# Three edits in the attention stage of a two-layer hybrid backbone: when bias tables are loaded, how a scan operand is laid out, and how many modulation products share an accumulator

## The chip, the cores and the metric

The kernel runs on one core of a Trainium2 chip. The time is device microseconds (us) of one execution; the number for the kernel before is the median of three runs. Rows of a trace come from one further execution, taken by the hardware profiler.

## The reference, cut to what matters

A backbone of two layers works on 1024 latent tokens and 256 context tokens of width 1024. Each layer computes six modulation vectors from two conditioning vectors, normalises the tokens, projects them into four head groups of width 256, mixes each group in its own way, and adds the projected result back; then a gated MLP follows. The three things that the change touches are these:

```
mod = split(silu(c) @ ada_w[l] + ada_b[l], 6)                    # 1024 x 6144 product, two rows
s_lat = q_r @ k_r.T * scale + bias ; s_lat = where(mask, s_lat, NEG_INF)   # neighbourhood heads
S = S*w_t + (S @ a_t) outer b_t + v_t outer k_t ; y_t = S @ r_t  # the scan, both directions
```

All results are float32, and one output of 1024 x 1024 is written.

## The kernel before, in words

**How the order is made.** The program is written as Python generators that are pulled in turns. A planner (the context is opened with `schedule_with_timeline_sim=True`) then fixes, at build time, the order of the instructions on each engine and on SP's queue, which issues all DMAs: of the instructions that its own model holds for ready, it takes the one that the program emitted first. An instruction that waits for nothing, as a load into a free buffer, can so come long before its place in the program. On the chip each engine works through its list in the planned order.

**The stage around the change.** `mix` first runs the dense projections and the preparation of the scan. Then it opens the attention units (`attn_open`, `units`, `unit_events`): per layer 8 units of the differential group, 20 or 16 of the latent group, and last 20 or 16 of the neighbourhood group (`na_unit`). A unit is 128 queries of a head pair: scores on PE (`sl`), row maxima on DVE (`rl`), exponentials on ACT (`ex`), transposes on PE (`tr`, into one of two `psT` buffers), products with V (`pv`), and an output DMA to `ymix` (L1068). While they run, `tick` pulls three side jobs at fixed rates: `scan` (`rw_step_gen`, rate 0.8), `ada` (`ada_gen`, rate 0.2, so one pull in five ticks) and, once `ada` has ended, `rwo` (`rw_out_gen`, rate 0.5, it ends with the stores at L784). Another job, `lanes_gen`, still does small DVE products (L547, L548) when the stage begins. The stage ends in the output projection, which reads `ymix` back.

**Bias.** In `na_unit`, `load()` brings Q (L865; three Q buffers, so a Q load waits until an earlier unit has let go) and calls `bias()` when the unit has another bias type than the one before. `bias()` loads a mask `msk` (L847, one buffer) and two bias tables `nb` (L850, two buffers) and adds the mask on POOL (L852, two additions). DVE uses them in the row maximum (L957). Each layer loads ten biases.

**Scan.** `rw_step_gen` does 20 steps per layer in sequence. A step multiplies on PE (L664, eight products, 128-row operands), copies the result to `Dt` on ACT (L667, 128 partitions), multiplies again (L676, eight products, each with operands of 64 rows, one half of the partitions for each head e of a pair), copies that result into the zero-padded `V1` in two halves, ACT for partitions 0 to 63 (L678) and DVE for 64 to 127 (L679), multiplies (L688), and updates the state on DVE (L696). POOL prepares `V1` and `stmp` (L660, L670) for it. The operands of a segment come by DMA (VS L629, SG L630, XB L631).

**Modulation.** `ada_gen` loads weights of 512 KB (L1535, three buffers), multiplies each (L1556, four column groups) and adds the 128x256 result to a row: ACT copies the first of eight (L1561), DVE adds the others (L1563). `adg` says how many of the eight accumulate in PSUM before the row is touched: here 1. The accumulator comes from `psT`. 48 weights are used in the first layer's stage, 32 in the second's; a load for weight j+3 is emitted right after the product of weight j.

Of the kernel before, what the change touches and what calls it, by code (L numbers as in the profile page):

```python
# [9 lines left out]
F32 = mybir.dt.float32  # L10
F32R = mybir.dt.float32r
AF = mybir.ActivationFunctionType
# [5 lines left out]
P = 128  # L18
# [22 lines left out]
class K:  # L41
# [561 lines left out]
    def rw_step_gen(self, l, pool, sgp, yp, psp, ptag, need_ctx, F):  # L603
        nc = self.nc
        TT, ACT, MM = nc.vector.tensor_tensor, nc.scalar.activation, nc.tensor.matmul
        segs = ([8, 9] + list(range(8)), [9, 8] + list(range(8))[::-1])
        sg = {}

        def need(i):
            return max(self.SLOT.index(segs[d][i]) for d in range(2))  # L610

        def step_y(i):
            return i >= 2 or need_ctx

        SZ = pool.tile([P, 2, 2, 2, 64], F32, name="SZ", bufs=1)
        for e in range(2):
            nc.gpsimd.memset(SZ[64 - 64 * e:128 - 64 * e, e], 0.0)

        def seg(i):
            SG = sgp.tile([P, 2, 1792], F32, tag="SG", name="SG", bufs=2)  # L620
            XB = pool.tile([P, 2, 4, 64], F32, tag="XB", name="XB", bufs=2)
            VS = pool.tile([P, 2, 2, 2, 2, 64], F32, tag="VS", name="VS", bufs=2)
            W = pool.tile([P, 2, 2, 2], F32, tag="W", name="W", bufs=2)
            for d in range(2):
                sl = self.SLOT.index(segs[d][i])
                vt = self.rvt[sl, d].rearrange("(c s) e p i -> e s c (p i)", c=2)
                for e in range(2):
                    q = slice(64 - 64 * e, 128 - 64 * e)
                    nc.sync.dma_start(VS[q, :, e, d].rearrange("s c p i -> s c (p i)"), vt[e])  # L629
                nc.sync.dma_start(SG[:, d], self.rsg[sl, d])  # L630
                nc.sync.dma_start(XB[:, d].rearrange("p u t -> p (u t)"), self.rxf[sl, d].rearrange("p u c t -> p (u c t)"))  # L631
                nc.gpsimd.tensor_copy(W[:, :, d], self.Wc[:, sl, d].rearrange("p (a c) -> p c a", a=2))
            if i == 0:
                for e in range(2):
                    nc.gpsimd.memset(VS[64 * e:64 * e + 64, 0, e], 0.0)
            BT = SG[:, :, 0:512].rearrange("p d (e u t) -> p d e u t", e=2, u=4)
            RB = SG[:, :, 512:768].rearrange("p d (u t) -> p d u t", u=4)
            ARM = SG[:, :, 768:1792].rearrange("p d (e u t) -> p d e u t", e=2, u=4)
            sg[i] = (XB, RB, BT, ARM, W, VS)

        while F["lanes"] <= need(0):
            yield
        seg(0)
        for _ in range(3):
            yield
        for step in range(20):
            i, c = step // 2, step % 2
            if c == 1 and i + 1 < 10:
                while F["lanes"] <= need(i + 1):
                    yield  # L650
            if c == 0 and i + 1 < 10 and F["lanes"] > need(i + 1):
                seg(i + 1)
            XB, RB, BT, ARM, W, VS = sg[i]
            V1 = pool.tile([P, 2, 2, 2, 64], F32, tag="V1", name="V1", bufs=2)
            pall = psp.tile([P, 2, 2, 2, 64], F32, tag=ptag, name="pall")
            pd, psa = pall[:, 0], pall[:, 1]
            tmp = pool.tile([P, 2, 2, 64], F32, tag="stmp", name="stmp", bufs=1)
            for e in range(2):
                q = slice(64 - 64 * e, 128 - 64 * e)
                nc.gpsimd.tensor_copy(V1[q, e], VS[q, c, e])  # L660
            for d in range(2):
                for p in range(2):
                    for e in range(2):
                        MM(pd[64 * e:64 * e + 64, d, p], ARM[:, d, e, 2 * p + c, 0:64], VS[:, c, e, d, p], start=True, stop=True)  # L664
            yield
            Dt = pool.tile([P, 2, 2, 64], F32, tag="Dt", name="Dt", bufs=2)
            ACT(Dt, pd, AF.Copy)  # L667
            for e in range(2):
                r = slice(64 * e, 64 * e + 64)
                nc.gpsimd.tensor_tensor(out=tmp[r], in0=VS[r, c, e], in1=W[r, c, :, :, None].to_broadcast([64, 2, 2, 64]), op=ALU.mult)  # L670
            yield
            for d in range(2):
                for p in range(2):
                    for e in range(2):
                        r = slice(64 * e, 64 * e + 64)
                        MM(psa[r, d, p], XB[r, d, 2 * p + c], Dt[r, d, p], start=True, stop=True)  # L676
            yield
            ACT(V1[0:64, 0], psa[0:64], AF.Copy)  # L678
            nc.vector.tensor_copy(V1[64:128, 1], psa[64:128])  # L679
            if step_y(i):  # L680
                for e in range(2):
                    nc.gpsimd.tensor_copy(SZ[64 * e:64 * e + 64, e], V1[64 * e:64 * e + 64, e])
            yield
            pss, py = pall[:, 0], pall[:, 1]
            for d in range(2):
                for p in range(2):
                    for e in range(2):
                        MM(pss[64 * e:64 * e + 64, d, p], BT[:, d, e, 2 * p + c], V1[:, e, d, p], start=True, stop=True)  # L688
            yield
            if step < 19:  # L690
                if c == 1 and i + 1 not in sg:
                    seg(i + 1)
                nVS = sg[i + c][5]
                for e in range(2):
                    r = slice(64 * e, 64 * e + 64)
                    TT(out=nVS[r, 1 - c, e], in0=tmp[r], in1=pss[r], op=ALU.add)  # L696
            yield
            if not step_y(i):
                yield
                continue  # L700
            for d in range(2):
                for p in range(2):
                    u = 2 * p + c
                    r = [slice(64 * e, 64 * e + 64) for e in range(2)]
                    for e in range(2):
                        MM(py[r[e], d, p], VS[:, c, e, d, p], ARM[:, d, e, u, 64:P], start=True, stop=False)
                    for e in range(2):
                        MM(py[r[e], d, p], SZ[:, e, d, p], RB[:, d, u], start=False, stop=True)
            yield
            if c == 0:  # L710
                yt = yp.tile([P, 2, 2, P], F32, tag="yt", name="yt", bufs=2)
            ACT(yt[:, :, :, c * 64:c * 64 + 64], py, AF.Copy)
            if c == 1:
                for d in range(2):
                    s = segs[d][i]
                    nc.sync.dma_start(self.ryd[d, :, :, s * P:(s + 1) * P], yt[:, d])
                F["seg"] = i
# [110 lines left out]
    def na_unit(self, l, pr, st, qi):  # L828
        nc, A = self.nc, self.A
# [13 lines left out]

        def bias():
            n = NW[ty]
            msk = kp.tile([P, 640], F32, tag="msk", name="msk")
            nc.sync.dma_start(msk[:, :n], A["na_mask"][:, NO[ty]:NO[ty] + n])  # L847
            b = kp.tile([P, 2, 640], F32, tag="nb", name="nb", bufs=2)
            ro = R0[ty] - QR[ty] + 7
            nc.sync.dma_start(b[:, :, 0:n], A["rpbp"][l, pr, :, :, ro * 64:ro * 64 + n])  # L850
            for h in range(2):
                nc.gpsimd.tensor_tensor(out=b[:, h, 0:n], in0=b[:, h, 0:n], in1=msk[:, 0:n], op=ALU.add)  # L852
            st["B"], st["ty"] = [b[:, 0], b[:, 1]], ty

        def load():
# [289 lines left out]
    def attn_open(self, l, qs, parts, pos, names, aside=None, between=None):  # L1145
# [5 lines left out]
        if self.kb[1] > 1:  # L1151
            d, na, m = us
            k = len(d)
            h = self.mixd
            a, b = d[:h], d[h:]
            us = [a + sum(([x, y] for x, y in zip(m, b)), []) + m[len(b):], na]
        sel, i = [], 0
# [4 lines left out]
        def gen():  # L1162
            for j, (k, cfg) in enumerate(parts):
                if not sel[j]:
                    continue
                if j and between:
                    between()
                cl = []
                self.psC = None
                for x, c in zip("ltvc", cfg):  # L1170
                    p, f = self.open(names[0] + x, c, None, PSUM) if c else (None, lambda: None)
                    cl.append(f)
                    setattr(self, "ps" + x.upper(), p)
                yield from self.slots(sel[j], pos)[0]
                for f in cl[::-1]:
                    f()
        n = sum(self.slots(x, pos)[1] for x in sel if x)

        def close():
            f2()  # L1180
            f1()
        return gen(), n, close

    def chain(self, order):
        for a, b in zip(order, order[1:]):
# [550 lines left out]
    kb = (2, 1)  # L1736
    adl = 6
    mixd = 3
    adg = 1
    adb = 3  # L1740
    rwb = ((2, 2), (1, 2))
    npd = 2
# [558 lines left out]
```

## Time and profile before

| | |
|---|---|
| median of 3 runs | 4302.95 us (4298.43 to 4312.81) |
| the profiled execution's own time | 4318.05 us |
| its span, first to last instruction | 4316.3 us |
| granted TensorE clock, mean | 0.955 |
| PE, DVE, ACT, POOL busy | 93%, 66%, 46%, 19% |

A row of a view names an instruction by its line, its engine, and the tiles it writes and reads (out<-in). PE is TensorE's matmul, DVE is VectorE, ACT is ScalarE, POOL is GpSimd, SPq is the queue of SyncE, which issues the DMAs. Times in a timeline are microseconds from the span's start. An idle time in brackets is that of the engine just before the instruction, with what ended it. PEclk is the granted share of 2.4 GHz.

### The profile page before, as it was taken

How to read it: one execution, taken by the hardware profiler on the slowest of the kernel's cores; microseconds unless marked ns; L12 is line 12 of the kernel's file. 1: busy time of each engine (PE TensorE's matmuls, PEld its weight loads, DVE VectorE, ACT ScalarE, POOL GpSimd, SP SyncE). 2: the span in 40 equal slices, each digit the busy share in tenths (PEclk: the TensorE clock that was granted, in tenths of full speed). 3: DMA queues.
4: the chain of work that ended last, by engine and by line, in shares of the span. 5: the costliest groups of instructions: out<-in, count | busy, mean ns of one | idle time of the engine just before them, and what ended most of it. 6: DMA issues, size and time to landing. Idle time of an engine off the chain costs nothing. (4 is left out here: it accounts for less than half of the span.)

```text
span 4316.3 us, 76712 instructions
## 1 busy us (share of the span) xinstructions
PE 4027.8 (93%) x29152; PEld 3319.9 (77%) x29152; DVE 2866.8 (66%) x5946; ACT 1982.7 (46%) x4386; POOL 801.9 (19%) x1320
## 2 busy tenths in 40 slices
PE   6999969999999999899998999969999999999998
PEld 4887856677777778788887887856677777788998
DVE  6577686656676765655556667686776766557666
ACT  4444435535554544433334444435545555435443
POOL 3244122212211112000001344122313111111000
PEclk7999979999999999999999999979999999999999
DMA  6444676655523243221213344687636332333332
GB/s 198 151 134 141 204 226 204 224 160 142 151 82 107 78 149 115 71 64 65 64 59 115 137 135 139 204 233 223 206 98 175 104 106 74 125 104 126 94 98 74
DMA packets 423199, 578.40 MB, mean 134 GB/s; under 512 B 109100, under 2 KB 287660, under 8 KB 421296
## 3 DMA queue, kind: packets, MB, share of 16 engines
q1 hardware_dynamic: 422832, 573.51, 42.9%
q8 instruction: 230, 3.77, 0.4%
q14 instruction: 137, 1.12, 0.1%
HBM read 433.47 MB, written 139.92 MB: 133 GB/s over the span
## 5 line engine op out<-in xcount | busy, mean ns | idle before, releaser
L141 PE MATMUL psm<-h_l,whi 128*128 128x512 f32 (+1 forms) x2112 | 710.3, 336 | 9.2 <-DVE h_l L258 9.0
L140 PE MATMUL psm<-h_h,whi 128*128 128x512 f32 (+1 forms) x2112 | 713.5, 338 | 2.3 <-ACT h_h L257 2.3
L142 PE MATMUL psm<-h_h,wlo 128*128 128x512 f32 (+1 forms) x2112 | 709.0, 336 | 0.0
L1888 DVE SCALAR_TENSOR_TENSOR x<-psm,mod,x 128x258 f32<-128x258 f32 (+2 forms) x616 | 327.0, 555 | 288.3 <-PE psm L142 287.9
L973 ACT ACTIVATE sm_P<-psL,sm_n 128x512 f32<-128x512 f32 (+1 forms) x672 | 392.8, 593 | 266.6 <-DVE sm_n L964 238.5
L141 PEld LDWEIGHTS psm<-h_l,whi 128*128 128x128 f32 x2112 | 399.4, 189 | 54.1 <-DVE h_l L258 12.0
L140 PEld LDWEIGHTS psm<-h_h,whi 128*128 128x128 f32 x2112 | 399.4, 189 | 52.0 <-DVE x L1888 4.0
L142 PEld LDWEIGHTS psm<-h_h,wlo 128*128 128x128 f32 x2112 | 399.1, 189 | 43.4 <-issue 0.2
L962 DVE TENSOR_REDUCE sm_m<-psL 128x1 f32<-128x512 f32 (+1 forms) x640 | 353.0, 578 | 88.0 <-PE psL L803 43.3
L140 PE MATMUL psm<-gh,dhi 128*128 128x510 f32 (+3 forms) x1056 | 364.8, 347 | 10.1 <-ACT mb L1852 5.1
L133 ACT ACTIVATE whi<-wst 128x1024 fp32r<-128x1024 f32 x176 | 186.6, 1060 | 401.2 <-PE psm L141 376.7
L141 PE MATMUL psm<-gl,dhi 128*128 128x510 f32 (+3 forms) x1056 | 357.7, 339 | 0.1
L142 PE MATMUL psm<-gh,dlo 128*128 128x510 f32 (+3 forms) x1056 | 357.4, 339 | 0.0
L134 DVE TENSOR_TENSOR wlo<-wst,whi 128x1024 fp32r<-128x1024 f32 x176 | 214.8, 1220 | 169.6 <-ACT whi L133 169.5
L1032 PE MATMUL psV<-PT,V 128*64 128x128 f32 x3488 | 299.3, 283 | 1.2 <-DVE sm_n L964 0.7
L1011 PE MATMUL psT<-ident,sm_P 128*128 128x128 f32 x1744 | 287.3, 287 | 10.6 <-DVE sm_P L1001 6.2
L1032 PEld LDWEIGHTS psV<-PT,V 128*64 128x64 f32 x3488 | 208.8, 137 | 83.7 <-issue 63.7
L1011 PEld LDWEIGHTS psT<-ident,sm_P 128*128 128x128 f32 x1744 | 206.4, 145 | 69.8 <-issue 29.7
L140 PEld LDWEIGHTS psm<-gh,dhi 128*128 128x128 f32 x1056 | 199.6, 189 | 44.6 <-ACT mb L1852 9.3
L142 PEld LDWEIGHTS psm<-gh,dlo 128*128 128x128 f32 x1056 | 200.2, 190 | 21.7
L141 PEld LDWEIGHTS psm<-gl,dhi 128*128 128x128 f32 x1056 | 200.4, 190 | 18.1 <-issue 0.7
L803 PE MATMUL psL<-K,Q 96*128 96x512 f32 (+1 forms) x400 | 148.8, 437 | 68.7 <-DMA Q<-dfq 34.4
(381 smaller groups left out, 9264.7 us busy)
## 6 DMA issues: line engine op xcount, KB each, us to landing
wst<-in_w_up_dram SPq DMA_DIRECT2D x176, 512.0 KB
wst<-in_w_down_dram SPq DMA_DIRECT2D x88, 512.0 KB
adw<-in_ada_w_dram SPq DMA_DIRECT2D x80, 512.0 KB
SG<-rsg SPq DMA_DIRECT2D x40, 896.0 KB
wst<-in_w_out_dram SPq DMA_DIRECT2D x96, 256.0 KB
rsg<-ARM SPq DMA_DIRECT2D x20, 1024.0 KB
K<-dfk SPq DMA_DIRECT2D x16, 960.0 KB
wst<-in_w_rw_dram SPq DMA_DIRECT2D x28, 512.0 KB
```

The source lines that it names most:

```text
L133: nc.scalar.activation(hi[:, :n], st[:, :n], AF.Copy)
L134: nc.vector.tensor_tensor(out=lo[:, :n], in0=st[:, :n], in1=hi[:, :n].bitcast(F32), op=ALU.subtract)
L140: mm(out, ah, bh, start=first, stop=False)
L141: mm(out, ah, bl, start=False, stop=False)
L142: mm(out, al, bh, start=False, stop=last)
L803: nc.tensor.matmul(ps, ld[0][0:96, j], ld[1][j // 2][0:96, j % 2, o:o + n], start=True, stop=True)
L962: nc.vector.tensor_reduce(out=m[:, j, i:i + 1], in_=src, axis=AX.X, op=ALU.max)
L973: ACT(Pt[:, off:off + n], s["L"][j][t][:, to:to + n], AF.Exp, bias=neg, accum_out=sm[:, j, i:i + 1])
L1011: nc.tensor.transpose(pt[:, j], Ph[:, (bb + j) * P:(bb + j + 1) * P], self.ident)
L1032: nc.tensor.matmul(s["po"][64 * h:64 * h + 64, 0], V[:, kts[i], h], s["PT"][h][:, i], start=i == 0, stop=i == nk - 1, tile_position=(0, 64 ...
L1888: STT(out=x[:, s:e], in0=ps[:, s:e], scalar=mod[:, v, 40 + m:41 + m], in1=x[:, s:e], op0=ALU.mult, op1=ALU.add)
```

## The change

`bias()` notes the last instruction emitted before it, which is the Q load of the same unit, and ties its two loads and two additions behind that instruction in the planner's order; the tie carries no semaphore. The scan's intermediate `Dt` becomes `DZ`, one buffer with an extra axis e, zeroed once where the other head's partitions are; ACT copies one half into it and DVE the other, and the second step's products take all 128 rows of XB against it. `adg` becomes 2: two weights accumulate in PSUM before the row is touched, and one pull does both.

```diff
-        SZ = pool.tile([P, 2, 2, 2, 64], F32, name="SZ", bufs=1)
-        for e in range(2):
-            nc.gpsimd.memset(SZ[64 - 64 * e:128 - 64 * e, e], 0.0)
+        DZ, SZ = (pool.tile([P, 2, 2, 2, 64], F32, name=n, bufs=1) for n in ("DZ", "SZ"))
+        for t in (DZ, SZ):
+            for e in range(2):
+                nc.gpsimd.memset(t[64 - 64 * e:128 - 64 * e, e], 0.0)
...
-            Dt = pool.tile([P, 2, 2, 64], F32, tag="Dt", name="Dt", bufs=2)
-            ACT(Dt, pd, AF.Copy)
+            ACT(DZ[0:64, 0], pd[0:64], AF.Copy)
+            nc.vector.tensor_copy(DZ[64:128, 1], pd[64:128])
...
-                        r = slice(64 * e, 64 * e + 64)
-                        MM(psa[r, d, p], XB[r, d, 2 * p + c], Dt[r, d, p], start=True, stop=True)
+                        MM(psa[64 * e:64 * e + 64, d, p], XB[:, d, 2 * p + c], DZ[:, e, d, p], start=True, stop=True)
...
         def bias():
             n = NW[ty]
+            last = nc.cur_bb.bb.instructions[-1]
+            first = len(nc.cur_bb.bb.instructions)
...
+            for i in nc.cur_bb.bb.instructions[first:]:
+                self.after(i, last)
...
+    def after(self, b, a):
+        self.tc.add_manual_dep(b, a.name, mybir.DependencyInfo(mybir.DependencyClass.NoSync, mybir.DependencyReason.DATA), reason="order")
...
-    adg = 1
+    adg = 2
```

## Rows read from the trace of the kernel before

**Rows 1.** The page: busy time and share of the span by engine.
```profile
PE 4027.8 (93%) x29152; PEld 3319.9 (77%) x29152; DVE 2866.8 (66%) x5946; ACT 1982.7 (46%) x4386; POOL 801.9 (19%) x1320
```
**Rows 2.** Busy time in stretches (stretch, length, PE, PEld, DVE, ACT, POOL, PEclk, DMA, GB/s).
```profile
590.00:1148.00 558.00, 497.54 (x5348) 369.98 (x5348) 379.81 (x1057) 268.13 (x799) 136.94 (x233) 0.91 0.65 190
600.00:640.00 40.00, 20.49 (x94) 12.11 (x94) 36.34 (x59) 14.40 (x43) 8.60 (x11) 0.50 0.94 279
...
2860.00:2900.00 40.00, 19.44 (x83) 10.90 (x85) 36.72 (x61) 13.79 (x42) 5.89 (x6) 0.50 0.95 293
```
**Rows 3.** Waits of PE, first layer's stage (us in total, times, longest us).
```profile
PE adaps L1556 <- DMA adw<-in_ada_w_dram: 11.8, 3, 6.4
PE psL L873 <- DVE sm_m L957: 3.3, 1, 3.3
...
PE pall L688 <- DVE V L679: 2.0, 4, 0.7
```
**Rows 4.** Waits of PE, second layer's stage.
```profile
PE adaps L1556 <- DMA adw<-in_ada_w_dram: 5.0, 3, 3.0
PE pall L688 <- DVE V L679: 4.2, 6, 1.4
PE psL L873 <- DVE sm_m L957: 4.0, 1, 4.0
PE pall L664 <- DMA VS<-rvt: 2.5, 1, 2.5
PE pall L676 <- ACT Dt L667: 1.6, 3, 0.5
```
**Rows 5.** The chain that ended last, in the second layer's stage (start, us, what).
```profile
2879.54 10.82 DMA nb<-in_rpbp_dram
...
2893.53 0.43 SPq L1535
...
2895.69 7.05 DMA msk<-in_na_mask_dram
...
2902.88 2.50 POOL nb L852 x2
...
3020.15 7.48 DMA adw<-in_ada_w_dram
```
**Rows 6.** Timeline, all engines: a scan step at the start of the first layer's stage.
```profile
629.87 1.12 PE L676 MATMUL pall<-Dt,XB 64*64 64x64 f32 x16 [0.48 <-ACT Dt L667]
631.03 0.38 ACT L678 ACTIVATE V<-pall 64x256 f32<-64x256 f32 x1 [1.22 <-PE pall L676]
...
631.45 0.43 DVE L679 COPY V<-pall 64x256 f32<-64x256 f32 x1 [0.30 <-ACT V L678]
...
634.87 1.08 PE L1556 MATMUL adaps<-adw,sc 128*32 128x256 f32 x8 [3.88 <-DMA adw<-in_ada_w_dram]
...
637.36 1.12 PE L688 MATMUL pall<-V,SG 128*64 128x64 f32 x16
```
**Rows 7.** Timeline of SP's queue: Q and bias loads, and a layer's last stores.
```profile
1012.18 0.54 SPq L865 DMA_DIRECT2D Q<-naq  x1
...
1118.80 0.55 SPq L850 DMA_DIRECT2D nb<-in_rpbp_dram  x1
...
3324.31 0.32 SPq L784 DMA_DIRECT2D ymix<-oy  x1
...
3349.47 0.32 SPq L1068 DMA_DIRECT2D ymix<-ot  x1
```
**Rows 8.** Timeline of DVE: the first use of a bias in the first layer.
```profile
1018.55 0.68 DVE L957 CUSTOM_DVE_ANT_0 sm_P<-psL,nb 128x512 f32<-128x512 f32 x1
```
**Rows 9.** Timeline of POOL: a bias load that waited for nothing but its transfer.
```profile
1122.96 2.52 POOL L852 TENSOR_TENSOR nb<-nb,msk 128x512 f32<-128x512 f32 x2 [7.32 <-DMA nb<-in_rpbp_dram]
```
**Rows 10.** The modulation accumulator by tile (ns min/median/max, first and last start, forms).
```profile
L1556 PE MATMUL adaps<-adw,sc x640: 376/403/637, 634.9 to 3071.7; 128*32 128x256 f32 x160
...
L1563 DVE TENSOR_TENSOR adarow<-adarow,adaps x70: 401/420/423, 647.3 to 3072.1; 128x256 f32<-128x256 f32 x70
```

## The prediction, made before the kernel was run

> **What bounds the kernel.** I read the page first. PE is busy 93% of the span and no other engine is above 66% [rows 1], so a microsecond counts only if PE works or waits in it. All three edits act in the attention stages, one for each layer, so I next cut the first one out with the view of busy time in stretches. There PE is busy 497.5 of 558 us and idle 60; DVE is busy 380, or 68% [rows 2]. The reader should see that even here little is to be won: the idle time of PE is all that an edit can take away as long as the products stay the same. The same view cut finer shows where it lies. In the first 40 us of the stage PE is busy half the time, at a granted clock of 0.50, while DVE is busy 36 of 40 us and the DMAs have a share of 0.94; the second layer's start is the same [rows 2]. Then I asked what PE waits for [rows 3, 4], and followed the chain of waits where the second layer's stage begins: it goes through bias loads [rows 5], although in the first layer the first bias is used at 1018.55, some 430 us after the stage's start at 590 [rows 2, 8].
>
> **The change part by part.**
>
> *Bias, at the start of a stage.* The planner now issues two biases at the head of the stage, because nothing holds their loads back. Behind the tie they come after the Q load of their own unit. What goes: on the chain of the second layer one transfer of nb of 10.82 us, one of the mask of 7.05 and two additions of 2.50 in sum [rows 5]. That these 20 us aren't saved whole has a reason in the rows: DVE, at 36 of 40 us, holds this stretch too [rows 2]. What PE itself waited for there is a scan operand, 2.5 us, once in each layer (two such rows, one shown [rows 4]), and the first modulation weight, 3.88 [rows 6] and 3.0 [rows 4]. Both loads stand behind the bias on SP's queue. I take the first wait whole, 5.0, and half of the second, 3.4, since two weights are needed then: -8.4 us. Ends: nothing, and -41 (20.4 twice).
>
> *Bias, where it is used.* In the first layer Q of the first neighbourhood unit is issued at 1012.18 [rows 7] and the first bias used at 1018.55 [rows 8], so there are 6.4 us for load and addition. A load when the DMAs had little else took 4.2 us from 1118.80 to 1122.96 [rows 7, 9], and the first addition takes half of 2.52; a load among others took 10.8 [rows 5]. That makes the use between 0.9 us early and 5.7 us late. The wait on the third bias, 3.3 and 4.0 us of PE [rows 3, 4], stays: it comes from there being two nb buffers, which the tie doesn't change. Behind the waiting addition POOL holds its scan and output work, behind the maximum DVE holds everything. I take +3 for both layers, with ends of 0 and +12.
>
> *Scan, second step.* PE has as many products. A burst of the 64-row step takes 1.12 us and a burst of the 128-row step L688 takes 1.12 us at the same granted clock [rows 6], so the padding costs PE nothing. The Trainium skill says otherwise in "TensorEngine Tiling (Array Packing)", Performance Considerations: contractions of 64 rows or less gain up to twice from row tiling, which this edit gives up; by that rule the step's bursts would double. The two rows disagree with the rule for this shape, and the measurement decides. What is added is a DVE copy of 0.43 us in each of 40 steps, 17.1 us of DVE in sum; ACT's copy keeps its length, since half the partitions take 0.38 [rows 6]. In V1 the DVE half began only once ACT's had ended, 631.41 to 631.45 [rows 6], so the new pair will stand one behind the other too. PE waited for the V1 pair 2.0 and 4.2 us, for Dt alone 1.6 in the second layer [rows 3, 4] and 0.5 in the first [rows 6]. If the new pair costs what V1's does, that is +4.1. Ends: 0 and +17, every copy on the path. A scan that ends later by some 20 x 0.43 = 9 us in a layer is covered: the side job behind it stores last at 3324, the attention units at 3349 [rows 7]. Without that cover the 9 us would be the stage's. Two more memsets on POOL in each layer stand where POOL waits anyway: nothing.
>
> *Modulation.* 40 of the 70 additions on DVE go (eight weights make one copy and three additions, not seven): 40 x 0.42 = -16.8 us of DVE [rows 10], which the new copies take back almost to the microsecond. With DVE at 68% I cost both at nothing. What counts is the loads. A pull now uses two weights, so the job needs half as many pulls. Now, in the second layer, 32 weights go from 2893.5 [rows 5] to 3071.7 [rows 10], 5.6 us a pull. The second weight of a pair is issued after the first product of the pair before, so its lead shrinks from three pulls to one, 5.6 us, while a landing took 7.48 us in the chain [rows 5]. PE's waits for weights are 16.8 us now [rows 3, 4]. 6.9 of it is counted above. The longest, 6.4, fell at the end of the first layer's job among other loads; the job will then be over, and I take it away: -6.4. The remaining 3.5 I double for the shorter lead: +3.5. Ends: 0, and (7.5 - 5.6) x 40 pairs = +76. The output job of the scan starts earlier, which only moves work.
>
> The sum: -8.4 + 3 + 4.1 - 6.4 + 3.5 = -4.2 us. It is made against the profiled execution, 4318.05 us, which stands 15.1 us above the median of the three runs; the difference is taken over to the median: 4302.95 - 4.2 = 4299. About 0.3%, or 13 us, is what a measurement of this kernel can tell from no change, so the forecast is no change.
>
> **The rivals.** *Slower: modulation weights that land too late.* The place is L1556, the price the bound above. It decides as soon as a landing takes longer than a pull: PE then stands at nearly every pair. For it: the stage's first 40 us have no DMA share left [rows 2], and a doubled job adds to that; the 7.48 us [rows 5]. Against: the planner puts other work first as far as its own model sees the delay, and three waits in a layer are few [rows 3, 4]. Half of the 76 us, with the rest of the sum as it is, makes -7.7 + 38 = +30, so 4333.
>
> *Faster: the start of the stage is worth what the chain says.* If the scan's first steps and the attention's start hang on the same queue, and DVE runs through its backlog sooner once its operands come, half of the 41 us is saved in place of 8.4: -20.5 + 4.2 = -16, so 4287, and down to 4266 at the whole of it. For it: PE's half clock in that stretch, which would end earlier too. Against: DVE's 36 of 40 us [rows 2].
>
> *Slower: padding costs PE.* If the doubled contraction took twice the 1.12 us after all, 40 x 1.12 = 45 us would be added, 4344. The row of L688 speaks against it [rows 6].
>
> *The tie does nothing.* Q loads could be planned early as well, and the biases with them. The buffers of Q speak against it: the first neighbourhood Q is issued at 1012 [rows 7]. Then the start's 8.4 and the use's 3 fall away: 4304, still no change, and its chance is in the forecast's.
>
> **How the numbers follow.** The forecast has 0.42, the faster rival 0.31, the late weights 0.24, the padding 0.03. So faster has 0.31, same 0.42, slower 0.27. The range reaches from the faster rival's far end, 4266, to a little past the late weights' middle, 4340, for some 0.1 is left out on either side.
>
> **What would show it.** Right: no bias load on SP before the first neighbourhood Q; the waits for the scan operand at the stage's start gone; L676's bursts as long as before; 30 DVE additions and a DVE copy that starts behind ACT's in each step; PE's waits for weights between 5 and 15 us; wait of PE on the third bias as now. Wrong: waits for weights above 30 us in sum (the slower rival), a first 40 us in which PE is busy 25 us or more (the faster one), L676 twice as long, or first bias maxima that wait over 6 us for POOL.

## The result, and the profile after

The changed kernel takes 4354.8 us (median of 4 runs, 4347.03 to 4362.33) against 4306.88 for the kernel before, measured beside it: a ratio of 1.0107, with a 95% interval of 1.0082 to 1.0131. That is 46 us slower (35 to 56), above the range that was given. The profiled execution took 4347.03 us, its span 4345.2.

The page of the kernel after, busy time by engine, answers to [rows 1]:

```profile
PE 4028.2 (93%) x29152; PEld 3326.5 (77%) x29152; DVE 2868.1 (66%) x5946; ACT 1982.2 (46%) x4386; POOL 809.1 (19%) x1324
```

PE is busy for the same 4028 us, and DVE for 2868 us in place of 2867. The 29 us between the two spans are idle time of PE. The view of busy time in stretches says where. First the two starts, which answer to [rows 2] (columns as there):

```profile
600.00:640.00 40.00, 23.24 (x174) 13.97 (x175) 34.33 (x58) 13.76 (x40) 6.48 (x12) 0.55 0.88 242
2870.00:2910.00 40.00, 23.14 (x125) 12.80 (x124) 36.05 (x63) 14.56 (x43) 3.48 (x8) 0.51 0.92 279
```

Then the middle of each stage (from 46 us after its first score product to 516 in the first layer, 456 in the second) and the 130 us behind that, which hold the stage's end. The kernel before:

```profile
642.00:1112.00 470.00, 439.28 (x4913) 329.79 (x4910) 309.98 (x896) 231.10 (x692) 120.72 (x211) 0.95 0.61 179
2906.00:3316.00 410.00, 387.22 (x4426) 294.76 (x4422) 285.78 (x811) 215.53 (x643) 111.54 (x197) 0.99 0.59 173
...
1112.00:1242.00 130.00, 122.73 (x760) 92.91 (x759) 89.50 (x206) 76.25 (x189) 15.37 (x21) 0.96 0.39 116
3316.00:3446.00 130.00, 123.85 (x764) 95.78 (x761) 90.96 (x206) 76.42 (x183) 13.55 (x17) 0.96 0.41 124
```

The kernel after:

```profile
640.00:1110.00 470.00, 427.33 (x4834) 329.29 (x4833) 306.71 (x885) 230.51 (x690) 120.19 (x208) 0.95 0.59 178
2915.00:3325.00 410.00, 381.16 (x4261) 291.51 (x4258) 277.91 (x765) 206.23 (x617) 105.73 (x189) 0.95 0.59 170
...
1110.00:1240.00 130.00, 113.92 (x712) 85.95 (x710) 82.83 (x194) 68.36 (x171) 15.23 (x18) 0.92 0.42 119
3325.00:3455.00 130.00, 117.47 (x766) 90.72 (x763) 86.27 (x228) 70.17 (x175) 20.11 (x23) 0.92 0.45 129
```

What PE loses in a stretch is its idle time, plus its busy time multiplied by what the granted clock lacks to 1. By that sum the starts lose 55.4 us after, 60.0 before (-4.6); the middles 111.9 against 79.3 (+33); the ends 47.1 against 23.3 (+24). The sum is rough, since it takes the mean clock of a long stretch for all of PE's busy time in it; made in pieces of 10 us it gives +34 for the middles and +19 for the ends. The starts became better, as intended. The loss is behind them. The parts add up to more than the 29 us between the spans: this trace of the kernel before lost some 11 us more ahead of the first stage, where the two kernels run in the same order (see the last section), and some 6 us more elsewhere.

What PE waits for in the first layer's stage of the kernel after (us in total, times, longest us), which answers to [rows 3]:

```profile
PE adaps L1563 <- DMA adw<-in_ada_w_dram: 17.9, 9, 4.5
...
PE psL L877 <- DVE sm_m L961: 8.1, 2, 6.6
...
PE pall L665 <- DMA VS<-rvt: 4.7, 1, 4.7
...
PE pall L688 <- DVE V L679: 1.1, 2, 0.7
PE pall L676 <- DVE DZ L668: 1.0, 2, 0.8
```

The second layer's, which answers to [rows 4]:

```profile
PE adaps L1563 <- DMA adw<-in_ada_w_dram: 11.2, 8, 3.4
...
PE psL L877 <- DVE sm_m L961: 3.3, 1, 3.3
PE pall L688 <- DVE V L679: 2.8, 2, 2.5
PE pall L665 <- DMA VS<-rvt: 2.4, 1, 2.4
PE pall L676 <- DVE DZ L668: 2.2, 5, 0.8
```

PE's waits for the scan's two copied operands, V and DZ, come to 7.1 us; for V and Dt they were 8.3. The new operand costs PE 3.2 us in waits, and yet it turns out to carry most of the loss. It shows on SP's queue, where the first layer's stage ends. Before:

```profile
1117.57 0.33 SPq L784 DMA_DIRECT2D ymix<-oy  x1
...
1126.08 0.96 SPq L796 DMA_DIRECT2D K<-dfk  x2
```

After:

```profile
1135.51 0.33 SPq L784 DMA_DIRECT2D ymix<-oy  x1
...
1139.69 0.90 SPq L796 DMA_DIRECT2D K<-dfk  x2
```

And on PE after:

```profile
1154.81 1.41 PE L803 MATMUL psL<-K,Q 96*128 96x512 f32 x3 [7.75 <-DMA Q<-dfq]
1161.07 0.80 PE L140 MATMUL pso<-h_h,wohi 128*128 128x512 f32 x1 [4.85 <-ACT h_h L1783]
```

The store at L784 is the last of the scan's output job. The loads of the next stage's keys come behind it, and PE stands 12.6 us at the boundary (7.75 and 4.85), where in the kernel before its waits there were 1.5 and 1.0.

### The profile page after: what moved, and what is told of

It reads as the page before. It is cut to its first block, busy times and chain, and to the rows that moved or that the text cites. A ratio compares the mean times of both kernels' runs of the same rounds, so it can differ in the third digit from the quotient of the medians.

```text
span 4345.2 us, 76611 instructions
## 1 busy us (share of the span) xinstructions
PE 4028.2 (93%) x29152; PEld 3326.5 (77%) x29152; DVE 2868.1 (66%) x5946; ACT 1982.2 (46%) x4386; POOL 809.1 (19%) x1324
## 5 line engine op out<-in xcount | busy, mean ns | idle before, releaser
L1025 ACT ACTIVATE PT<-psT 128x512 f32<-128x512 f32 (+2 forms) x300 | 151.7, 525 | 142.8 <-PE psT L1015 139.9
```

The costliest lines, as they stand in the source:

```text
L1025: ACT(dst, src, AF.Copy)
```

## The experiments

All ratios are against the kernel before, timed on the same chip in the same session.

### Each part alone

The three parts were put into the kernel before one by one, and the first two together; the edits are those of the diff above.

> Only the tie of the bias loads. The changed kernel's two attention stages, taken from the first score product after the stage's start to the first product of the output projection, last 16.2 and 22.7 us longer than before (567.6 against 551.4, 514.1 against 491.4). Three theories share that out. Scan theory: the added DVE copy makes the scan's steps longer (17.4 and 17.3 us from step to step against 15.8 and 14.4), the last store of the scan's output comes 21 and 25 us later against the stage's start, and the loads of the next stage stand behind it on SP. By it the tie alone is worth -10 to +5 us. Weights theory: two modulation weights for a product, with the same three buffers, halve the lead of the loads (waits of PE on weights 29.8 us in sum against 17.4) and it is this that slows PE and scan; by it too the tie alone is worth -10 to +5. Tie theory: the biases come late where they are used (waits of PE on the maximum of a neighbourhood score 11.4 us against 7.3) and the order of the start is worse; by it the tie alone costs +15 or more.

> Only the zero-padded operand of the scan's second step, with its copy split between ACT and DVE. Scan theory: nearly the whole loss is here, +25 to +50 us; steps of 17 us or more in both stages, the last store of the scan's output 15 us or more later against the stage's start, and a wait of PE for the next stage's loads at the end of the stage. Weights theory: -3 to +10, steps within 0.6 us of those before. Tie theory: the same -3 to +10.

> Only the modulation products in pairs. Weights theory: +25 to +50 us, waits of PE on weights near 30 us in sum, scan steps of 17 us or more although the scan's code is that of before. Scan theory: -10 to +12 us: the waits on weights rise by the 12 us that the changed kernel shows or less, and 40 additions fewer on DVE and an earlier end of the job give some of it back; scan steps within 0.6 us of those before.

> The changed kernel without its pairs: tie and padded operand. Scan theory: +20 to +50 us, as the padded operand alone. Weights theory: -8 to +8 us. If the parts only act together (each alone within 10 us of before, and this one too), the loss belongs to the pairs on top of a stretched scan.

| kernel | ratio (95%) | us |
|---|---|---|
| tie alone | 1.0035 (1.0022 to 1.0047) | +15 |
| padded operand alone | 1.0072 (1.0054 to 1.0089) | +31 |
| pairs alone | 1.0011 (0.9997 to 1.0025) | +5 |
| tie and padded operand | 1.0100 (1.0082 to 1.0117) | +43 |

Two thirds of the loss come with the padded operand, as the scan theory had it; pairs by themselves are worth nothing that can be measured, although their scan steps (16.4 and 15.4 us) are 0.7 and 1.0 us longer than before, more than that theory allowed. The tie's 15 us weren't expected by it.

### Padding or hop?

The padded operand brings products of 128 rows, one buffer in place of two, and a copy on DVE behind the copy on ACT. Two kernels part these.

```diff
 padded operand, ACT alone:
-            nc.vector.tensor_copy(DZ[64:128, 1], pd[64:128])
+            ACT(DZ[64:128, 1], pd[64:128], AF.Copy)
 no padding, copy split:
-            ACT(Dt, pd, AF.Copy)
+            ACT(Dt[0:64], pd[0:64], AF.Copy)
+            nc.vector.tensor_copy(Dt[64:128], pd[64:128])
```

> The padded operand alone, but both halves copied by ACT, one after the other, so that the products have 128 rows and DVE has no part in the copy. Hop theory: what cost the 31 us of the padded operand alone is the DVE copy in the scan's chain: it began 0.72 and 0.84 us after ACT's copy on average and took 0.43, 1.2 us in each of 40 steps. A second ACT copy takes 0.38 and doesn't wait for DVE's queue, so about a third stays: +4 to +16 us. Padding theory: the cost is in the products with 128 rows or in the single DZ buffer (Dt had two): still +22 to +38.

> The kernel before with Dt as it was (64 rows for each product, two buffers, no zeros), only its copy split: ACT takes rows 0 to 63, DVE rows 64 to 127. Hop theory: +20 to +38 us, the DVE copy again starting behind ACT's. Padding theory: -6 to +8 us.

Padded with ACT alone: 1.0012 (0.9997 to 1.0027), +5 us. Split copy without any padding: 1.0067 (1.0047 to 1.0088), +29 us. It is the hop to DVE. The view of the tile that the kernel after pads (ns min/median/max, first and last start) shows the price of its pieces; the first row stands for the products:

```profile
L676 PE MATMUL pall<-DZ,XB x640: 219/222/370, 624.8 to 3226.8; 128*64 128x64 f32 x160
L667 ACT ACTIVATE DZ<-pall x40: 365/377/378, 622.9 to 3222.8; 64x256 f32<-64x256 f32 x40
L668 DVE COPY DZ<-pall x40: 427/428/428, 623.4 to 3224.3; 64x256 f32<-64x256 f32 x40
```

The same view of the kernel before, for its Dt:

```profile
L676 PE MATMUL pall<-Dt,XB x640: 218/218/367, 629.9 to 3166.9; 64*64 64x64 f32 x160
L667 ACT ACTIVATE Dt<-pall x40: 380/383/408, 629.4 to 3163.6; 128x256 f32<-128x256 f32 x40
```

A product of 128 rows takes 222 ns, one of 64 rows 218, and a step's burst of 16 takes 0.69 us where it took 0.68 (both at the full clock; 1.12 in both at the half clock). Half the partitions take ACT 377 ns, all of them 383: the split saves nothing. One step in the timeline of the kernel after:

```profile
657.73 0.38 ACT L667 ACTIVATE DZ<-pall 64x256 f32<-64x256 f32 x1 [0.84 <-PE pall L665]
658.60 0.43 DVE L668 COPY DZ<-pall 64x256 f32<-64x256 f32 x1
...
659.58 0.55 PEld L676 LDWEIGHTS pall<-DZ,XB 128*64 128x64 f32 x16 [0.17 <-issue]
659.58 0.69 PE L676 MATMUL pall<-DZ,XB 128*64 128x64 f32 x16
```

In the built program each DVE half carries a wait for ACT, and in all 40 steps it starts only after ACT's has ended; where DVE is at other work it comes later still. Whether the wait is there for the PSUM tile that both read or for the tile that both write was not tried. Over the 20 steps of a layer of the padded kernel the DVE copy began 0.72 us (first layer) and 0.84 us (second) after the end of ACT's on average, and took 0.43: 1.15 and 1.27 us for each of 40 steps, 48 us of scan in both layers together. The Trainium skill says in "PSUM — Partial Sum Buffer", PSUM bank collisions raise a hardware error, that two engines may be in one bank at once as long as they are in different groups of 32 partitions, as these halves are; no run here shows it, since the wait is in every kernel that splits a copy.

Cut as above, the ends of the padded kernel's stages lose 59.0 us, 36 more than before:

```profile
1121.00:1251.00 130.00, 114.52 (x615) 85.10 (x615) 83.20 (x165) 68.27 (x159) 15.95 (x21) 0.91 0.42 124
3322.00:3452.00 130.00, 111.23 (x634) 83.65 (x634) 78.07 (x188) 63.05 (x156) 18.41 (x20) 0.87 0.43 118
```

Its middles, worked out in the same way, lose 11 less. A table shows the way from the scan to the ends (us after the stage's first score product; first layer / second layer; the last scan step is taken at the last product of L676; the last column by the sum of the section on the result):

| kernel | last scan step | last output store | next K load | PE's loss at the end |
|---|---|---|---|---|
| before | 334 / 307 | 521 / 465 | 530 / 471 | 12 / 11 |
| padded operand alone | 361 / 334 | 538 / 486 | 544 / 496 | 26 / 33 |
| split copy, no padding | 359 / 335 | 539 / 489 | 546 / 499 | 27 / 31 |
| after | 363 / 358 | 542 / 489 | 546 / 494 | 25 / 22 |
| padded operand, ACT alone | 345 / 321 | 532 / 468 | 536 / 473 | 27 / 24 |
| pairs alone | 347 / 328 | 526 / 456 | 534 / 461 | 24 / 16 |

The last two rows lose more at the ends too, 28 and 17 us, and yet the two kernels cost 5 us each by their timed runs; their middles lose 9 and 12 less than before, and the execution that was traced of the former took 4327.58 us, 15 above that kernel's median. So a later end is a price, but part of it can come back in the middle, and the loss at the end of a single trace is not the loss of the kernel.

Scan and output job share the one PSUM buffer of pool `apr`, and half of the output job's eight latent pieces wait for the scan's last segment; the output job's pool is closed before the next stage opens its own. In all 18 kernels of this study and both layers the K loads come 4 to 10 us after the last output store. That it is the memory which ties them is read from the code and was not tried by itself.

### Would pulling the scan earlier help?

```diff
-    rates = dict(ada=0.2, prep=0.8, lanes=0.5, scan=0.8, mla=1.5, rwo=0.5)
+    rates = dict(ada=0.2, prep=0.8, lanes=0.5, scan=1.0, mla=1.5, rwo=0.5)
```

> The whole changed kernel with one number changed: the scan is pulled 1.0 times a tick in place of 0.8. If the loss is made real by the scan's output job ending late, with the next stage's loads behind its last store on SP, then an earlier scan brings it back where the program's order holds the scan: last stores of its output 10 us or more earlier, 12 us or more faster than the changed kernel (under 4343 us). If the chain of the scan's own copies and products sets its pace, whatever the program's order, steps stay at 17 us and the time within 8 us of the changed kernel's 4355.

1.0104 (1.0086 to 1.0123), the same as the changed kernel; steps of 16.8 and 17.0 us, the last output store no earlier. Pulling the scan more often does not shorten it; that its own chain of copies and products sets the pace fits with this.

### The tie's 15 us

> The tie alone and only in the second layer. The tie in both layers cost 15 us, but its two attention stages lasted 552.9 and 488.2 us against 551.4 and 491.4; its trace has one wait of PE of 20.1 us at 1767 us, long after the first stage, before the first product of the MLP into psm, where before has 9.5 us in three waits. Accident theory (the plan after the stage came out with that product's PSUM buffer still being read by the norm): the tie in the second layer alone costs nothing, -6 to +6 us. Tie theory (late biases, worse order): about half of 15, +5 to +12.

1.0012 (0.9997 to 1.0027): +5 us, which lies in both expected ranges and decides nothing. The 20 us wait in the trace of the tie alone:

```profile
1766.96 0.55 PE L140 MATMUL psm<-h_h,whi 128*128 128x256 f32 x1 [20.11 <-DVE nt L253]
```

In the kernel before the same product waits for nothing:

```profile
1743.38 0.56 PE L140 MATMUL psm<-h_h,whi 128*128 128x256 f32 x1
```

In the built programs the product's tile `psm` lies on PSUM bank 0 in both. The tile `pb` of the norm just ahead, which DVE reads until 1766.8, lies on bank 1 in the kernel before and on bank 0 in the tied one, so the product waits for the whole norm. It lies on bank 1 in the changed kernel too. The banks can be swapped by hand:

```diff
+        if self.swap:                    # l == 0 and the last token group
+            d = self.pn.tile([P, 512], F32, tag=self.pnt, name="psz")
+            nc.vector.memset(d[:, 0:1], 0.0)
         pb = self.pn.tile([P, 512], F32, tag=self.pnt, name="pb")
...
+        if self.swap:
+            nc.vector.tensor_copy(d[:, 1:2], pb[:, 0:1])
```

> The tie in both layers, as in the run that cost 15 us, and in the norm of the last token group of the first layer's MLP a PSUM tile more (one written element, kept until the norm's broadcast product is issued), so that this product's bank and the bank of its statistics change places: the broadcast lies on bank 1 again, as in the kernel before, and the next MLP product, on bank 0, has not to wait for it. Accident theory: the 20.1 us wait is back to some 9.5 in all, and the tie costs nothing: -5 to +6 us against before. Tie theory: still +10 to +18.

> The kernel before with the same PSUM tile more at the same place and nothing else: here it puts the broadcast of the norm on bank 0, where the next MLP product is to go. Accident theory: the loss of the tied kernel without any tie, +9 to +18 us, with one wait of PE near 20 us before the first product into psm. Tie theory: -3 to +4.

Tie with the banks swapped back: 0.9997 (0.9983 to 1.0011), -1 us. The kernel before with the banks swapped: 1.0025 (1.0010 to 1.0039), +11 us, and its row

```profile
1768.00 0.55 PE L140 MATMUL psm<-h_h,whi 128*128 128x256 f32 x1 [20.18 <-DVE nt L260]
```

So the tie is worth nothing by itself, and its 15 us were an accident of the plan 600 us behind its stage, which the changed kernel does not have. Nor does the kernel with tie and padded operand: PE's longest wait before a product into `psm` is 5.2 us in its first layer. Its 43 us are therefore not 31 and 15, but 31 and 12 that the accident does not explain.

### What is left without the hop

> The whole changed kernel with the two halves of the padded operand both copied by ACT, and the same PSUM tile more (without it this plan puts the broadcast on bank 0 too). If the DVE hop is the changed kernel's loss, what is left is the second ACT copy (5 us measured by itself) and the pairs (5 us measured by themselves): -2 to +14 us against before. If the parts cost something together that none costs alone (the changed kernel lost more in the middle of its stages, and less at their ends, than tie and padding without the pairs): +18 to +32.

> The changed kernel with the modulation job pulled 0.1 times a tick in place of 0.2, so that weights are wanted at the old pace. In the middle of its two stages (from 45 us after the start on) the changed kernel loses about 34 us more of PE's time, idle or at the half clock, than before, and at their ends 19 us more. Weights theory: the middle's loss is from weights wanted twice as fast; at the old pace it goes, 15 us or more faster than the changed kernel (under 4340 us). Hop theory: the scan's length is set by the hop all the same, what is saved in the middle comes back at the ends, within 10 us of the changed kernel.

The changed kernel with both halves copied by ACT, and the broadcast on bank 1: 1.0057 (1.0034 to 1.0079), +25 us: 21 gained, but more left than the parts add up to. With the modulation job at half the rate: 1.0109 (1.0091 to 1.0127), no change. Waits of PE on weights fell from 29.1 to 18.0 us and the time stayed: with the middles' loss smaller by 14 us and the ends' larger by 7 (each worked out in pieces of 10 us), what was saved in the middle came back at the ends in part, and the rest does not show in the time.

> Tie and pairs, without the padded operand (this plan leaves the norm's broadcast on bank 1, so the 20 us wait is not in it). With the DVE hop taken out the changed kernel still lost 24 us, where its parts by themselves add up to 10. If tie and pairs together make it (bias loads behind Q loads meet weights wanted twice as fast): +12 to +25. If it takes the longer scan: -4 to +9.

> Padded operand and pairs, without the tie. Sum of the parts: 31 and 5, +36. If pairs and the longer scan together make the extra loss (the pairs put scan, weights and output job into the same stretch of DVE and PE): +42 to +58, with the scan's steps at 17 us or more. If the tie is needed for it: +26 to +40.

Tie and pairs: 1.0042 (1.0028 to 1.0056), +18 us, where the tie by itself is worth -1 (with the broadcast on bank 1, as here) and the pairs +5. Padded operand and pairs: 1.0081 (1.0060 to 1.0102), +35, the sum of the two. The tie makes the difference, and not only beside the pairs. The kernels without it and with it are (us against before; none of these traces has the 20 us wait):

| kernel | without the tie | with it |
|---|---|---|
| padded operand | +31 | +43 |
| padded operand and pairs | +35 | +46 |
| pairs | +5 | +18 |
| V1 copied by ACT alone (next section) | -12 | 0 |
| nothing else (with it: the banks swapped back) | 0 | -1 |

One difference is uncertain by some 10 us, but four of four are 11 to 13. So the changed kernel's 46 us are, within these intervals, the hop's 31, the pairs' 5, and some 12 that the tie costs in company and not alone. Where the 12 come from stays open. In the traces the tie raises the loss of the middles in these four kernels (by 16, 44, 30 and 30 us, by the sum of the section on the result) and lowers it alone (by 12); with the pairs about half of it lies in the first 100 us behind the starts, where the weights are wanted. The bias shows a part, here in the kernel after, first layer: the second bias waits for its mask, which has one buffer, on POOL, and DVE waits for POOL:

```profile
1029.91 2.48 POOL L854 TENSOR_TENSOR nb<-nb,msk 128x512 f32<-128x512 f32 x2 [8.54 <-DMA msk<-in_na_mask_dram]
```

```profile
1031.21 0.69 DVE L961 CUSTOM_DVE_ANT_0 sm_P<-psL,nb 128x512 f32<-128x512 f32 x1 [7.67 <-POOL nb L854]
```

With tie and pairs PE waits 8.7 us on such maxima in that stage (8.1 in the kernel after) and 4.3 to 4.4 with the tie alone: 4 us, as far as PE's waits tell. A second mask buffer or a fourth weight buffer, which would part the causes, was not tried.

### The other way round

V1 is copied in two halves in the kernel before already [rows 6]. If a hop costs, taking that one out should gain.

```diff
-            nc.vector.tensor_copy(V1[64:128, 1], psa[64:128])
+            ACT(V1[64:128, 1], psa[64:128], AF.Copy)
```

> The other way round: the kernel before with the copy of V1, which is split between ACT and DVE already, made by ACT alone. The DVE half waits 0.52 and 0.86 us behind ACT's and takes 0.43, so a step should lose some 0.6 to 0.9 us and the scan 12 to 18 us in a layer. If the scan's chain sets the end of the stage in the kernel before too: -6 to -20 us, the last store of its output and the next stage's K loads 8 us or more earlier. If the kernel before has the scan covered: within 5 us of before, and the loss at the ends of the stages, 21.6 us, no smaller.

> The tie with V1 copied by ACT alone (here too the broadcast stays on bank 1). Tie without the 20 us wait measured -1 us, and its start of the stages lost 5 us less; with a shorter scan behind it: -4 to -20 us if the scan sets the end, -5 to +4 if not. This is the candidate to beat both kernels.

Alone: 0.9971 (0.9959 to 0.9983), 12 us faster than before, the fastest kernel of the study. The scan ends 18 and 12 us earlier (316 and 295 us after the stage's first product), the next K loads come at 510 and 451, 20 us earlier. The time and the stores came as the first of the two theories said. The loss at the ends did not shrink, though, as by that theory it should have (35 us by the same sum, 23 before); PE lost less in the middles, 45 against 79 us:

```profile
645.00:1115.00 470.00, 453.96 (x5163) 343.98 (x5160) 317.33 (x945) 255.62 (x764) 123.39 (x213) 0.98 0.63 187
2885.00:3295.00 410.00, 397.83 (x4468) 301.91 (x4464) 283.06 (x812) 226.45 (x671) 113.19 (x199) 0.98 0.62 181
```

(In the four other kernels that have the scan as before and the pairs not, with the tie or with swapped banks, the middles lose 67 to 77, so a part of the 79 belongs to the one trace.) Taking a hop out gains, then, but where it gains is not where putting one in costs; why was not followed. With the tie: 1.0000 (0.9985 to 1.0015), the last but one row of the table above.

## Why the prediction was wrong

**Scan, second step.** This is the term that failed: +4.1 us, with an upper end of 17, and the whole hop costs 31. Three things were wrong in it. It was priced by PE's waits at V1's products, as if a step were paid where its product stands; but between the scan's products PE has other work, so a longer step hardly appears as a wait, but as a later scan. PE's waits on DZ are 3.2 us after, on Dt they were 2.1. The upper end took the copy's 0.43 us and left out the wait before it, 0.7 to 0.8 us in the padded kernel: the one V1 pair that was read began 0.04 us behind ACT's [rows 6], while over V1's 40 steps of the kernel before the mean is 0.52 and 0.86 us. And the cover wasn't one: the output job's last store at 3324 was compared with the attention's last store at 3349 [rows 7], when what stands behind the former is the next stage's K load, at 3331 in the kernel before. In the padded kernel the scan's last step comes 27 us later in each layer (9 and 6 of them there at the first step already), the K loads 15 and 25 us later, and PE loses 36 us more at the boundaries. "Without that cover the 9 us would be the stage's" named the right danger with too small a number.

**Padding** costs PE nothing: 222 ns against 218 a product, 0.69 us against 0.68 a burst. The rival that had the sign and nearly the time, 4344 for padding that doubles the step, had the wrong cause. The prediction cites the Trainium skill for it, "TensorEngine Tiling (Array Packing)": that page names row tiling for contractions of 64 rows under Performance Considerations, and the gain of up to twice in its Overview, under Theoretical Speedup. That gain was not seen here, by 640 products of either kind.

**Bias at the start of a stage.** The loads went behind the first neighbourhood Q as expected (in the first layer Q is issued at 1005.31, its mask at 1005.89), and the starts lose 4.6 us less where 8.4 were taken. But neither wait went that was named: those on the scan operand are 4.7 and 2.4 us, 7.1 where it was 5.0 (and in the first layer the view of the kernel before names no transfer for its 2.5, only issue), and those on the first two weights 5.8 where it was 6.9. What became better is that PE has more to do in those stretches, 46.4 us against 39.9. That the size came near is in part luck.

**Bias where it is used.** +3 was taken; PE's waits on maxima rose from 7.3 to 11.4, +4.1. The size of these waits was right, the place was not: the first bias's maxima wait 2.2 us on DVE and none on PE, and it is the second's that wait 7.67 and 6.6, for the one mask buffer, where the wait on the third bias was said to stay. That a tie in the plan can move a PSUM bank 600 us later was in no term, and cost 15 us in the kernel that has it; that the tie costs some 12 us beside another edit was in none either.

**Modulation.** DVE's additions fell from 70 to 30, and DVE's busy time stayed what it was, 2868 against 2867 us, as was said:

```profile
L1570 DVE TENSOR_TENSOR adarow<-adarow,adaps x30: 409/420/422, 638.1 to 3030.6; 128x256 f32<-128x256 f32 x30
```

The waits for weights, forecast at 5 to 15 us, are 29.1, so the term's -6.4 did not come and the shorter lead costs more than 3.5. Alone it is paid back: with the pairs alone the job's last load is issued 106 and 50 us earlier in its stage, and the output job, which starts after it, has its first store 16 us after the scan's last step in place of 26 in the first layer, and 30 us before it in the second. That fits with the measured +5 (-1 to +11). The rival of late weights had +30; its sign was right for the whole change and its cause was not: at the old pace of weights the time is the same. Together with the tie it costs 18, which no term had.

## What to carry to other kernels

A serial chain that runs beside a busy engine can have its price at the chain's end and not in the waits of that engine: multiply what is added to a step, queue time included, by the steps (48 us here, of which 31 were paid), and look for what starts when the chain is over. Before a copy is split between two engines, see whether the program lets both run at once; here it didn't, one engine on all partitions was as fast as on half of them, and the second engine added 1.2 us. Two edits that each cost little can cost more together: time the pairs too. Before a change is judged by a small loss, see whether the plan has moved something far away: a wait of 20 us that is not near the edit is a reason to swap the placement by hand and time again.

## What was not expected of the hardware

On every engine the order of the first 585 us is the same in the plans that were compared, yet in the profiled runs the first attention stage began between 592.2 and 605.0 us. A difference of 12 us between two single traces need not come from an edit, and the ratios above rest on the timed runs.

A stall costs more than its length. In the kernel after, the stretches of 10 us around the boundary are

```profile
1140.00:1150.00 10.00, 5.89 (x66) 4.24 (x65) 4.17 (x15) 3.87 (x11) 0.00 (x0) 1.00 1.00 229
1150.00:1160.00 10.00, 1.41 (x3) 0.83 (x3) 0.00 (x0) 0.00 (x0) 0.00 (x0) 0.56 1.12 255
1160.00:1170.00 10.00, 8.93 (x31) 6.91 (x32) 8.14 (x15) 8.11 (x16) 0.00 (x0) 0.76 0.57 213
```

PE is idle for 12.6 us and then works with a granted clock of 0.76 in a stretch in which it is nearly always busy: another 2 us of work lost. At the ends of the padded kernel's stages such clock takes up to 25 us of the 59, by the same rough sum.
